# A transformer block kernel: norm columns as stationary operand, x in fewer transfers, modulation issued a block earlier

## The chip, the cores and the metric

The kernel runs on one core of a Trainium2 chip. The metric is the device time of one execution in microseconds (us), lower being better; it is given as the median of several runs. One further execution was recorded by the hardware profiler, and all rows of the trace come from that one.

## The reference

One layer of a diffusion backbone over 512 latent tokens, with 256 context tokens as a prefix, width 1024, all in fp32. Cut to what matters here:

```python
def rmsnorm(x, g):
    return x * lax.rsqrt(jnp.mean(x * x, axis=-1, keepdims=True) + EPS) * g

mod = jax.nn.silu(c) @ w_mod + b_mod                 # c_ctx likewise
sh1, sc1, gt1, sh2, sc2, gt2 = jnp.split(mod, 6)
h = rmsnorm(x, g_norm_mix) * (1.0 + sc1) + sh1       # x: 512 x 1024
hc = rmsnorm(ctx, g_norm_mix) * (1.0 + csc1) + csh1  # ctx: 256 x 1024
mix = token_mixer(h, hc, ...)   # h @ w_in, attention and a gated recurrence, @ w_out
x = x + gt1 * mix
h2 = rmsnorm(x, g_norm_ffn) * (1.0 + sc2) + sh2
x = x + gt2 * swiglu(h2, w_gate, w_up, w_down)
return rmsnorm(x, g_final)
```

The norm needs, for every token, the root of a mean over the 1024 features, and the modulation needs a product of a vector with the matrix `w_mod` before the first large product, `h @ w_in`, can begin.

## The kernel before, in words

Activations lie transposed, with features on the 128 partitions and tokens along the free axis: `xs` is x as 8 blocks (k) of 128 features by 512 tokens, `xc` the context as 8 blocks of 256 tokens. Each large product is made of three (`mm3`, lines 148 to 152: L150, L151, L152): operands are split into a rounded high part and a low part (`hh` and `hl` for h, `gh` and `gl` for the context, `wh` and `wl` for weights). A weight unit of 128 x 1024 is loaded by DMA into `wf`; ACT casts it to `wh` (L132) and DVE subtracts to get `wl` (L133).

**The start.** TensorE runs 32 idle products on a tile of ones (`warm`, L351). x comes in eight transfers (L255, L256), then the modulation weights `wms`, weight units and the context in the order of a written list (L267). ACT squares each block of x (L307) and DVE adds it to the accumulator `acl` (L309). The sum over the 128 partitions is a product on TensorE: the accumulator, 128 tokens at a time, is the stationary operand, two columns of ones move (`rstd_sums`, L174), so each group of 128 tokens gets its sum as one column. `rstd_cols` makes 1/root from it: ACT takes the square root (L190), DVE the reciprocal and one Newton step that ends in L182. To have the value of each token on all partitions, `rstd_diag` multiplies the identity matrix with each column (L209 on DVE, L207 on ACT, in turn), and `rstd_spread` multiplies that diagonal from the left with ones (L216), into a PSUM bank.

**The modulation.** `modvec(k)` multiplies two weight tiles for block k with the vectors of c and c_ctx (eight products on bands of 32 partitions, L320) and copies the result to an SBUF tile `spk` or `modsb` in turn (L323). `modsel(k)` picks the bands by two small products with a selection matrix (L329) and makes scale and shift, `ab`, in three DVE steps (the group L332 is one of them). `make_h` then makes block k of h: DVE multiplies x by scale and 1/root (L339), ACT adds the shift and rounds to `hh` (L340), DVE subtracts to get `hl` (L341).

**The value projection.** The loop from L376 (`g0`) runs over the eight blocks of 128 features. Each has twelve 512-column products, for four groups of 128 tokens (`big` banks, token groups 0 to 3), written in three calls of `g0_mm`. Between them stand, for the next block, `modsel` and `make_h`, and `modvec` for the one after. The context is squared at k = 1, its norm is at k = `lag` - 2 and `lag` - 1 with `lag` = 4, its blocks of h follow two per step, and its products lag four steps behind. The order on each engine is not this order alone: a scheduler in the framework places instructions by priorities and estimated times, so that the code's order and an engine's differ. When the loop ends, the banks are copied out and the other projections, the attention, the recurrence, the output projection and the FFN follow.

**Later norms.** `norm2` (L960) norms x behind the output projection, in two halves of 256 tokens, beside products of the output projection and the FFN. `final` (L1041) norms the result; for the second half it is the last thing that the kernel does: sums, `rstd_cols`, `rstd_diag`, spread, eight multiplications on DVE and the transfers out.

Of the kernel before, what the change touches and what calls it, by code (L numbers as in the profile page):

```python
# [10 lines left out]
F32 = mybir.dt.float32  # L11
# [3 lines left out]
AF = mybir.ActivationFunctionType  # L15
ALU = mybir.AluOpType
AX = mybir.AxisListType

P = 128
# [33 lines left out]
def block_kernel(ctx: ExitStack, tc: tile.TileContext, xT, ctxT, vec, cin, cst, msk, wm, wmt, wi, wqkv, wo, wgu, wd, out):  # L53
# [8 lines left out]
    def nm(s):  # L62
        uid[0] += 1
        return f"{s}_{uid[0]}"
# [137 lines left out]
    def rstd_diag(tp, cols):  # L202
        r, nb = cols
        dg = tp.tile([P, 4, P], F32, tag="rs_d", name=nm("rsd"), bufs=1)
        for b in range(nb):
            if b % 2:
                nc.scalar.activation(dg[:, b, :], ident, AF.Copy, scale=r[:, b : b + 1])  # L207
            else:
                nc.vector.tensor_scalar(dg[:, b, :], ident, r[:, b : b + 1], None, op0=ALU.mult)  # L209
        return dg, nb  # L210

    def rstd_spread(diag):
        dg, nb = diag
        pb = sm()
        for b in range(nb):
            nc.tensor.matmul(pb[:, b * P : (b + 1) * P], ones, dg[:, b, :], start=True, stop=True,  # L216
                             skip_group_check=True)
        return pb

    def rstd_bcast(tp, sqs, ntok, dim, fast=False):  # L220
        return rstd_spread(rstd_diag(tp, rstd_cols(tp, rstd_sums(sqs, ntok), dim, fast)))
# [33 lines left out]
    for k in range(KT):  # L255
        nc.sync.dma_start(xs[:, k, :], xT[:, k, :])  # L256
# [47 lines left out]
    def squares(src, acc_, n):  # L304
        for k in range(KT):
            sq_ = temp(n) if k else acc_
            nc.scalar.activation(sq_, src[:, k, :], AF.Square)  # L307
            if k:
                nc.vector.tensor_add(acc_, acc_, sq_)  # L309

    squares(xs, acl, NL)
# [37 lines left out]
    def warm(n):  # L349
        for _ in range(n):  # L350
            nc.tensor.matmul(pw[:, :P], ones, ones, start=True, stop=True, skip_group_check=True)  # L351
# [12 lines left out]

# [10 lines left out]
    lag = 4  # L375
    for k in range(max(KT, lag + KT // 2)):  # L376
        if k < KT:
            g0_mm(k, (0,))
        if k + 1 < KT:
            abs_.append(modsel(k + 1, sb))  # L380
            make_h(xs, rl, NL, k + 1, abs_[k + 1], 0, hh, hl)
# [4 lines left out]
        if k == lag - 1:  # L386
            rc = rstd_spread(rstd_diag(A, ccols))
# [653 lines left out]
    def final(a):  # L1041
        w = 256
        dg = rstd_diag(N2, rstd_cols(N2, rstd_sums(sqa[a], w), DM, fast=True))
        yield
        pb = rstd_spread(dg)
# [119 lines left out]
```

## Time and profile before

| | us |
|---|---|
| median of three runs | 793.04 (790.87 to 794.18) |
| profiled execution | 792.44 |
| its span in the trace | 790.6 |
| start up to 20.9 | 20.9, TensorE busy 17.10 |
| 20.9 to 71.4, value projection | 50.5, TensorE busy 47.79 |
| 71.4 to 780, all the rest but the tail | 708.6, TensorE busy 700.07 |
| 780 to 790.6, tail | 10.6, TensorE busy 2.02 |

The profiled execution takes 1.84 us more than its span, before the first and behind the last instruction that the trace shows. PE is TensorE, PEld its weight load, DVE VectorE, ACT ScalarE, POOL GpSimd, SP the engine that issues most transfers. A row of the timeline gives start and duration in us, engine, line, operation, out<-in by the program's names, shape and count; in square brackets the idle time of the engine just before it and the instruction that ended it. An fp32 product shows as two passes, so that four products read x8. A row of the windows view gives for each engine the busy time and the count of instructions, then the clock that was granted to TensorE (1.00 is full speed), the share of DMA engines busy and GB/s. A row of the groups gives the shape, the count, the busy time in all and the mean in ns, then the idle time before and who ended it.

### The profile page before, as it was taken

How to read it: one execution, taken by the hardware profiler on the slowest of the kernel's cores; microseconds unless marked ns; L12 is line 12 of the kernel's file. 1: busy time of each engine (PE TensorE's matmuls, PEld its weight loads, DVE VectorE, ACT ScalarE, POOL GpSimd, SP SyncE). 2: the span in 40 equal slices, each digit the busy share in tenths (PEclk: the TensorE clock that was granted, in tenths of full speed). 3: DMA queues.
4: the chain of work that ended last, by engine and by line, in shares of the span. 5: the costliest groups of instructions: out<-in, count | busy, mean ns of one | idle time of the engine just before them, and what ended most of it. 6: DMA issues, size and time to landing. Idle time of an engine off the chain costs nothing.

```text
span 790.6 us, 10838 instructions
## 1 busy us (share of the span) xinstructions
PE 767.0 (97%) x4342; PEld 630.8 (80%) x4342; DVE 445.0 (56%) x819; ACT 307.2 (39%) x564; POOL 10.1 (1%) x18
## 2 busy tenths in 40 slices
PE   8899999999999989999999999999999999999995
PEld 7568878788887768888999888888888888888885
DVE  4686569739778988984566434432333233223324
ACT  5344245434554576664344223222322222212211
POOL 0000000000000100000000000000000000000000
PEclk8999999999999999999999999999999999999997
DMA  8924723321110022453503354423232333332303
GB/s 326 396 82 142 238 81 107 133 67 61 48 55 28 28 96 98 133 166 148 160 2 107 107 159 133 149 92 107 80 107 82 104 78 96 93 100 82 111 2 107
DMA packets 26708, 88.78 MB, mean 112 GB/s; under 512 B 2977, under 2 KB 5281, under 8 KB 26530
## 3 DMA queue, kind: packets, MB, share of 16 engines
q1 hardware_dynamic: 25570, 87.04, 33.5%
q10 hardware_dynamic: 1088, 1.05, 0.4%
q8 instruction: 34, 0.56, 0.3%
q14 instruction: 16, 0.13, 0.0%
HBM read 85.97 MB, written 2.10 MB: 111 GB/s over the span
## 4 chain that ended last, share of the span: by engine, by line
PE 86%; DVE 7%; DMA 4%; ACT 2%; issue 1%; SPq 0%; DVEq 0%; ACTq 0%
PE big L150 17%; PE big L151 16%; PE big L152 16%; PE sm L150 9%; PE sm L151 9%; PE sm L152 9%; PE big L861 2%; DMA xc<-in_ctxT_dram 1%; PE sm L606 1%; DMA wm<-in_wm_dram 1%; PE big L862 1%; DMA wms<-in_wm_dram 1%; PE sm L880 1%; DVE U L587 1%; PE sm L600 1%
## 5 line engine op out<-in xcount | busy, mean ns | idle before, releaser
L133 DVE TENSOR_TENSOR wl<-wf,wh 128x1024 fp32r<-128x1024 f32 (+2 forms) x100 | 119.6, 1196 | 184.5 <-ACT wh L132 184.3
L132 ACT CAST wh<-wf 128x1024 fp32r<-128x1024 f32 (+2 forms) x100 | 102.9, 1029 | 279.8 <-PE big L151 167.4
L150 PE MATMUL big<-h2h,wh 128*128 128x512 f32 (+1 forms) x368 | 140.3, 381 | 0.0
L151 PE MATMUL big<-h2l,wh 128*128 128x512 f32 (+1 forms) x368 | 140.0, 381 | 0.0
L152 PE MATMUL big<-h2h,wl 128*128 128x512 f32 (+1 forms) x368 | 140.0, 381 | 0.0
L151 PEld LDWEIGHTS big<-h2l,wh 128*128 128x128 f32 x368 | 69.2, 188 | 14.6
L152 PEld LDWEIGHTS big<-h2h,wl 128*128 128x128 f32 x368 | 69.2, 188 | 14.5
L150 PEld LDWEIGHTS big<-h2h,wh 128*128 128x128 f32 x368 | 69.2, 188 | 14.4
L150 PE MATMUL sm<-ah,wh 128*128 128x512 f32 (+1 forms) x198 | 73.5, 371 | 0.0
L152 PE MATMUL sm<-ah,wl 128*128 128x512 f32 (+1 forms) x198 | 73.4, 371 | 0.0
L151 PE MATMUL sm<-al,wh 128*128 128x512 f32 (+1 forms) x198 | 73.4, 370 | 0.0
L427 DVE SCALAR_TENSOR_TENSOR wl<-wl,cs 128x1024 f32<-128x1024 f32 x32 | 39.0, 1220 | 35.0 <-DMA wl<-in_wmt_dram 35.0
L150 PEld LDWEIGHTS sm<-ah,wh 128*128 128x128 f32 x198 | 37.3, 188 | 7.1
L151 PEld LDWEIGHTS sm<-al,wh 128*128 128x128 f32 x198 | 37.3, 188 | 7.1
L152 PEld LDWEIGHTS sm<-ah,wl 128*128 128x128 f32 x198 | 37.3, 188 | 7.1
L150 PE MATMUL big<-hh,wh 128*128 128x512 f32 x104 | 42.8, 411 | 0.0
L150 PE MATMUL big<-wh,hh 128*128 128x512 f32 x96 | 39.4, 414 | 3.3 <-ACT hh L340 1.9
L151 PE MATMUL big<-hl,wh 128*128 128x512 f32 x104 | 40.9, 394 | 0.0
L152 PE MATMUL big<-hh,wl 128*128 128x512 f32 x104 | 40.9, 393 | 0.0
L151 PE MATMUL big<-wl,hh 128*128 128x512 f32 x96 | 38.2, 400 | 0.0
L152 PE MATMUL big<-wh,hl 128*128 128x512 f32 x96 | 38.1, 399 | 0.0
L508 DVE RECIPROCAL G<-S 128x528 f32<-128x528 f32 x8 | 27.5, 3433 | 0.1
(320 smaller groups left out, 1345.9 us busy)
## 6 DMA issues: line engine op xcount, KB each, us to landing
wf<-in_wgu_dram SPq DMA_DIRECT2D x44, 512.0 KB, 3.4
wl<-in_wmt_dram SPq DMA_DIRECT2D x32, 512.0 KB, 3.5
wf<-in_wi_dram SPq DMA_DIRECT2D x25, 512.0 KB, 4.2
wf<-in_wd_dram SPq DMA_DIRECT2D x16, 512.0 KB, 3.5
wms<-in_wm_dram SPq DMA_DIRECT2D x11, 512.0 KB, 9.6
wf<-in_wo_dram SPq DMA_DIRECT2D x8, 512.0 KB, 3.3
wf<-in_wd_dram SPq DMA_DIRECT2D x8, 384.0 KB, 3.1
wm<-in_wm_dram SPq DMA_DIRECT2D x5, 512.0 KB, 10.2
```

What stands on the lines that cost most here:

```text
L132: nc.scalar.copy(hi[:, :w], f[:, :w])
L133: nc.vector.tensor_sub(lo[:, :w], f[:, :w], hi[:, :w].bitcast(F32))
L150: nc.tensor.matmul(o, lh, rh, start=start, stop=False, skip_group_check=True)
L151: nc.tensor.matmul(o, lh, rl, start=False, stop=False, skip_group_check=True)
L152: nc.tensor.matmul(o, ll, rh, start=False, stop=stop, skip_group_check=True)
L427: nc.vector.scalar_tensor_tensor(f, f, 1.0, sc, op0=ALU.mult, op1=ALU.mult, accum_out=acc)
L508: nc.vector.reciprocal(I, S)
L587: nc.vector.scalar_tensor_tensor(U[:, c1, :], U[:, c0, :], er[:, 1, c0 : c0 + 1], U[:, c1, :], op0=ALU.mult, op1=ALU.add)
L600: nc.tensor.matmul(t, a2[:, j, :], vt[:, j, h * P : (h + 1) * P], start=True, stop=False, skip_group_check=True)
L606: nc.tensor.matmul(t[g * CH : (g + 1) * CH, :], qg[:, c, :], U[:, c, :], start=False, stop=(g == 1 and d == 1), skip_group_check=True, til ...
L861: nc.tensor.matmul(ps[:, 0, :], L, R[:, :NL], start=(i == 0), stop=(i == 4), skip_group_check=True)
L862: nc.tensor.matmul(ps[:, 1, :NC], L, R[:, NL:], start=(i == 0), stop=(i == 4), skip_group_check=True)
```

## The change

Six edits go together.

1. The diagonals are gone. `rstd_spread` takes the column of 1/root itself as the stationary operand, the same column repeated 128 times (a broadcast view), and the identity moves. The result is the same spread. It applies in all norms (start, context, `norm2`, `final`).
2. x comes in four transfers of two blocks, not eight of one; in the list of later loads the second weight unit comes one place earlier (102 ahead of 6 and -1).
3. The eighth square of x isn't added on DVE; `rstd_sums` takes accumulator and last square, so that TensorE adds them: eight products, not four.
4. Modulation: the code gets `next_h` (selection and h of the next block) and `next_mod` (the next vector), and in blocks 0 and 1 each is called a second time, so that from block 1 on they are a block further ahead.
5. The context's products lag five steps, not four, and its norm moves with them.
6. Idle products: 30, not 32, ahead of the sums (`warm`), two between the first vector and its selection, and five behind the spread (`warm_on`, which multiplies a given tile with ones into a bank that nobody reads).

```diff
-    def rstd_spread(diag):
-        dg, nb = diag
+    def rstd_spread(cols):
+        r, nb = cols
         pb = sm()
         for b in range(nb):
-            nc.tensor.matmul(pb[:, b * P : (b + 1) * P], ones, dg[:, b, :], start=True, stop=True,
+            nc.tensor.matmul(pb[:, b * P : (b + 1) * P], r[:, b : b + 1].to_broadcast([P, P]), ident, start=True, stop=True,
                              skip_group_check=True)
...
-    for k in range(KT):
-        nc.sync.dma_start(xs[:, k, :], xT[:, k, :])
+    for k in range(0, KT, 2):
+        nc.sync.dma_start(xs[:, k : k + 2, :], xT[:, k : k + 2, :])
...
-    for step in (2, 101, 4, 6, -1, 102, 8, -2, 10, 12, 103, 14, 16):
+    for step in (2, 101, 4, 102, 6, -1, 8, -2, 10, 12, 103, 14, 16):
...
             nc.scalar.activation(sq_, src[:, k, :], AF.Square)
+            if last and k == KT - 1:
+                return sq_
...
-    warm(32)
-    cols = rstd_cols(A, rstd_sums([acl], NL), DM, fast=True)
-    sb = modvec(0)
-    dg = rstd_diag(A, cols)
-    abs_ = [modsel(0, sb)]
-    pb = rstd_spread(dg)
+    def warm_on(t, n):
+        for _ in range(n):
+            nc.tensor.matmul(pw[:, :P], ones, t, start=True, stop=True, skip_group_check=True)
+
+    warm(30)
+    cols = rstd_cols(A, rstd_sums([acl, sql], NL), DM, fast=True)
+    sbs = [modvec(0)]
+    warm_on(sbs[0][:, :P], 2)
+    abs_ = [modsel(0, sbs[0])]
+    pb = rstd_spread(cols)
+    warm_on(cols[0][:, 0:1].to_broadcast([P, P]), 5)
     make_h(xs, pb, NL, 0, abs_[0], 0, hh, hl)
     nc.scalar.copy(rl, pb)
-    sb = modvec(1)
...
+    def next_h():
+        k = len(abs_)
+        if k < KT:
+            abs_.append(modsel(k, sbs[k]))
+            make_h(xs, rl, NL, k, abs_[k], 0, hh, hl)
+
+    def next_mod():
+        if len(sbs) < KT:
+            sbs.append(modvec(len(sbs)))
...
-    lag = 4
+    lag = 5
     for k in range(max(KT, lag + KT // 2)):
         if k < KT:
             g0_mm(k, (0,))
-        if k + 1 < KT:
-            abs_.append(modsel(k + 1, sb))
-            make_h(xs, rl, NL, k + 1, abs_[k + 1], 0, hh, hl)
+        if k >= 1:
+            next_h()
...
             g0_mm(k, (1,))
-            if k + 2 < KT:
-                sb = modvec(k + 2)
+            next_mod()
             g0_mm(k, (2, 3))
+            if k < 2:
+                next_h()
+                next_mod()
...
     def final(a):
         w = 256
-        dg = rstd_diag(N2, rstd_cols(N2, rstd_sums(sqa[a], w), DM, fast=True))
+        cols = rstd_cols(N2, rstd_sums(sqa[a], w), DM, fast=True)
         yield
-        pb = rstd_spread(dg)
+        pb = rstd_spread(cols)
```

`norm2` changes like `final`. What follows shows how the instructions stand on three stretches; the numbers in the names tell one buffer from another. Lines of the changed code have moved: the warm-up is L340, `warm_on` L344, the modulation vector L309, the selection L318, the spread L206, a square L294.

TensorE from the warm-up to the first product of the value projection, before:

```order
L351 MATMUL sm_25_194<-ones_63 128x128 x32
L174 MATMUL sm_26_227<-ones_63,acl_168 128x2 x4
L320 MATMUL sm_30_241<-wms_1_77,csil_94 32x256 x8
L329 MATMUL sm_32_256<-cs_61,spk_76 128x2 x2
L216 MATMUL sm_34_263<-rsd_31_251,ones_63 128x128 x4
L320 MATMUL sm_36_273<-wms_1_77,csil_94 32x256 x4
L150 MATMUL big_38_284<-wh_7_110,hh_85 128x512
```

and of the change, from the last two of the eight sums on:

```order
L174 MATMUL sm_26_220<-ones_63,acl_164 128x2
L174 MATMUL sm_26_220<-ones_63,t512_24_183 128x2
L309 MATMUL sm_30_238<-wms_1_77,csil_94 32x256 x8
L344 MATMUL sm_25_189<-spk_76,ones_63 128x128 x2
L318 MATMUL sm_31_250<-cs_61,spk_76 128x2 x2
L206 MATMUL sm_33_257<-cs_61,rsr_29_231 128x128 x4
L344 MATMUL sm_25_189<-rsr_29_231,ones_63 128x128 x5
L309 MATMUL sm_37_280<-wms_1_77,csil_94 32x256 x4
L150 MATMUL big_35_272<-wh_7_106,hh_85 128x512
```

Two idle products now stand between the vector and its selection, and five between the spread and the second vector's first half; the spread reads `rsr`, the column, where it read `rsd`, the diagonals.

TensorE from block 0 to block 1 of the value projection, before (`big_38` and `big_39` are the banks, `modsb_37` the copied vector of block 1):

```order
L152 MATMUL big_38_284<-wh_7_110,hl_86 128x512
L150 MATMUL big_38_284<-wh_7_110,hh_85 128x512
L151 MATMUL big_38_284<-wl_8_111,hh_85 128x512
L329 MATMUL sm_40_289<-cs_61,modsb_37_282 128x2 x2
L152 MATMUL big_38_284<-wh_7_110,hl_86 128x512
L152 MATMUL big_39_285<-wh_7_110,hl_86 128x512
L320 MATMUL sm_42_302<-wms_2_78,csil_94 32x256 x4
L150 MATMUL big_39_285<-wh_7_110,hh_85 128x512
L151 MATMUL big_39_285<-wl_8_111,hh_85 128x512
L152 MATMUL big_39_285<-wh_7_110,hl_86 128x512
L320 MATMUL sm_42_302<-wms_3_79,csil_94 32x256 x4
L150 MATMUL big_38_284<-wh_7_110,hh_85 128x512
```

and of the change, where the banks are `big_35` and `big_36` and the vector is `modsb_38`:

```order
L309 MATMUL sm_37_280<-wms_2_78,csil_94 32x256 x3
L151 MATMUL big_36_273<-wl_8_107,hh_85 128x512
L152 MATMUL big_36_273<-wh_7_106,hl_86 128x512
L150 MATMUL big_36_273<-wh_7_106,hh_85 128x512
L151 MATMUL big_36_273<-wl_8_107,hh_85 128x512
L152 MATMUL big_36_273<-wh_7_106,hl_86 128x512
L318 MATMUL sm_39_297<-cs_61,modsb_38_289 128x2 x2
L309 MATMUL sm_41_307<-wms_2_78,csil_94 32x256 x4
L309 MATMUL sm_41_307<-wms_3_79,csil_94 32x256 x4
L150 MATMUL big_35_272<-wh_7_106,hh_85 128x512
```

The selection for block 1 stood behind seven products of block 0, five of them following it; now all twelve stand ahead of it, and only the two halves of a vector lie between it and the first product of block 1.

ACT around the context norm, before (`wh_14` is the third weight unit, of which block 4 makes the first use, `acc` the context's accumulator and later its spread):

```order
L340 ACTIVATE hh_85<-t512_53_383,ab_52_379 128x512
L190 ACTIVATE rsr_57_392<-sm_54_387,epst_64 128x2
L207 ACTIVATE rsd_61_431<-cs_61,rsr_57_392 128x128
L388 COPY acc_169<-sm_62_434 128x256
L340 ACTIVATE hh_85<-spk_76,ab_60_424 128x512
L340 ACTIVATE gh_87<-sp256_75,ab_33_259 128x256
L340 ACTIVATE gh_87<-sp256_75,ab_41_292 128x256
L132 CAST wh_14_135<-wf_13_133 128x1024
```

and of the change:

```order
L329 ACTIVATE hh_85<-t512_49_373,ab_48_369 128x512
L294 ACTIVATE sp256_75<-xc_93 128x256
L329 ACTIVATE hh_85<-spk_76,ab_55_399 128x512
L190 ACTIVATE rsr_64_445<-sm_61_440,epst_64 128x2
L132 CAST wh_14_131<-wf_13_129 128x1024
L329 ACTIVATE hh_85<-t512_60_436,ab_59_432 128x512
L390 COPY acc_165<-sm_72_491 128x256
```

The cast of that unit stood behind the context's spread and two of its blocks; now it stands right behind the square root of the context's norm, which waits for the context's sums.

More of the change, by code (lines that the diff above doesn't have):

```diff
@@ L200, in rstd_cols @@
         return r, n
-    def rstd_diag(tp, cols):
+    def rstd_spread(cols):
         r, nb = cols
[L204 to L210, printed above, removed]
-    def rstd_spread(diag):
-        dg, nb = diag
         pb = sm()
         for b in range(nb):
-            nc.tensor.matmul(pb[:, b * P : (b + 1) * P], ones, dg[:, b, :], start=True, stop=True,
+            nc.tensor.matmul(pb[:, b * P : (b + 1) * P], r[:, b : b + 1].to_broadcast([P, P]), ident, start=True, stop=True,
                              skip_group_check=True)
         return pb
-    def rstd_bcast(tp, sqs, ntok, dim, fast=False):
-        return rstd_spread(rstd_diag(tp, rstd_cols(tp, rstd_sums(sqs, ntok), dim, fast)))
     D = pool("D", "right")
@@ L303, in block_kernel, with squares @@
     acc = A.tile([P, NC], F32, name="acc")
-    def squares(src, acc_, n):
+    def squares(src, acc_, n, last=False):
         for k in range(KT):
@@ L307, in squares @@
             nc.scalar.activation(sq_, src[:, k, :], AF.Square)
+            if last and k == KT - 1:
+                return sq_
             if k:
                 nc.vector.tensor_add(acc_, acc_, sq_)
-    squares(xs, acl, NL)
+    sql = squares(xs, acl, NL, last=True)
     rl, rc = acl, acc
@@ L386, in block_kernel @@
         if k == lag - 1:
-            rc = rstd_spread(rstd_diag(A, ccols))
+            rc = rstd_spread(ccols)
             nc.scalar.copy(acc, rc[:, :NC])
@@ L1042, in final @@
         w = 256
-        dg = rstd_diag(N2, rstd_cols(N2, rstd_sums(sqa[a], w), DM, fast=True))
+        cols = rstd_cols(N2, rstd_sums(sqa[a], w), DM, fast=True)
         yield
-        pb = rstd_spread(dg)
+        pb = rstd_spread(cols)
         for n in range(KT):
```

## The prediction

> **What bounds the kernel now.** I read the page first, then the windows view, then the timeline of the first 72 us and of the last 10. The page: how busy TensorE is, and the clock it was granted.
>
> ```profile
> span 790.6 us, 10838 instructions
> PE 767.0 (97%) x4342; PEld 630.8 (80%) x4342; DVE 445.0 (56%) x819; ACT 307.2 (39%) x564; POOL 10.1 (1%) x18
> PEclk8999999999999999999999999999999999999997
> ```
>
> TensorE is busy for 97% of the span. The change edits the first 70 us and the two later norms, so its worth is the TensorE time not lost there, plus the tail. The profiled execution took 792.44 us: the span of 790.6 and 1.84 around it. It lies 0.6 below the median of the runs, 793.04. About 0.5% (4.0 us) is what a measurement of this kernel can tell from no change, so "faster" means below 789.1 and "slower" above 797.0.
>
> The windows view of stretches cut where the granted clock changes; the columns are the stretch, its length, busy us of PE, PEld, DVE, ACT and POOL, then clock, DMA share and GB/s.
>
> ```profile
> 10.22:13.63 3.41, 1.80 (x17) 1.61 (x16) 2.22 (x4) 2.42 (x3) 0.00 (x0) 1.00 1.02 419
> 13.63:17.04 3.41, 2.86 (x23) 1.51 (x22) 1.54 (x8) 1.89 (x4) 0.00 (x0) 0.50 1.03 413
> 17.04:20.46 3.42, 3.27 (x18) 2.16 (x18) 1.61 (x5) 0.35 (x1) 0.00 (x0) 0.50 1.03 412
> 34.11:37.52 3.41, 2.12 (x12) 1.49 (x10) 2.53 (x9) 1.14 (x2) 0.00 (x0) 1.00 1.03 410
> 778.21:781.62 3.41, 2.06 (x18) 1.89 (x16) 1.39 (x5) 0.68 (x2) 0.00 (x0) 1.00 0.78 257
> 8.00:10.00 2.00, 2.00 (x20) 2.00 (x19) 1.71 (x3) 1.87 (x4) 0.00 (x0) 1.00 1.03 357
> ```
>
> The clock is halved for two stretches of 3.41 us, 13.63 to 20.46, and comes back. The stretch ahead of them had 1.80 us of busy TensorE, but 0.8 of that are two-column sums. 34.11 to 37.52 was hardly busier (2.12), with 512-column products, and kept the clock. 778.21 to 781.62 had 2.06, half of it two-column sums, and the page's last slice shows the clock lower. I read from this that two-column products hardly hold the clock up.
>
> The timeline of the norm of x, up to the first projection product (start, duration, instruction, idle before and who ended it):
>
> ```profile
> 1.06 10.13 PE L351 MATMUL sm<-ones 128*128 128x128 f32 x64 [1.06 <-DVE epst L90]
> 10.78 0.63 ACT L307 ACTIVATE t<-xs 128x512 f32<-128x512 f32 x1
> 11.27 0.69 DVE L309 TENSOR_TENSOR acl<-acl,spk 128x512 f32<-128x512 f32 x1
> 12.06 0.69 DVE L309 TENSOR_TENSOR acl<-acl,t 128x512 f32<-128x512 f32 x1
> 12.81 1.15 PE L174 MATMUL sm<-ones,acl 128*128 128x2 f32 x8 [1.61 <-DVE acl L309]
> 13.89 1.93 PE L320 MATMUL sm<-wms,csil 128*32 128x256 f32 x16
> 14.96 0.16 DVE L182 SCALAR_TENSOR_TENSOR rsr<-rst,rsr 128x4 f32<-128x4 f32 x1
> 15.89 0.42 DVE L323 COPY spk<-sm 128x256 f32<-128x256 f32 x1 [0.76 <-PE sm L320]
> 16.23 0.47 DVE L209 TENSOR_SCALAR rsd<-cs,rsr 128x128 f32<-128x128 f32 x2
> 16.37 1.01 PE L329 MATMUL sm<-cs,spk 128*128 128x2 f32 x4 [0.55 <-DVE spk L323]
> 17.24 2.05 PE L216 MATMUL sm<-rsd,ones 128*128 128x128 f32 x8
> 19.33 0.75 DVE L339 SCALAR_TENSOR_TENSOR t<-xs,ab,sm 128x512 f32<-128x512 f32 x1 [1.43 <-PE sm L216]
> 20.11 0.72 ACT L340 ACTIVATE hh<-t,ab 128x512 fp32r<-128x512 f32 x1 [3.33 <-DVE t L339]
> 20.89 0.73 PE L150 MATMUL big<-wh,hh 128*128 128x512 f32 x2 [0.58 <-ACT hh L340]
> ```
>
> What ends last is the modulation vector's products at half clock (1.93), its copy, the selection (1.01), the spread (2.05), then 1.6 of DVE and ACT. The projection starts at 20.89.
>
> From there to the end of the value projection the timeline has three waits of TensorE; the other rows give unit prices at full clock:
>
> ```profile
> 26.42 0.50 PE L150 MATMUL big<-wh,hh 128*128 128x512 f32 x1
> 31.01 0.49 PE L150 MATMUL big<-wh,hh 128*128 128x512 f32 x1 [1.08 <-ACT wh L132]
> 37.41 0.50 PE L150 MATMUL big<-wh,hh 128*128 128x512 f32 x1 [1.29 <-ACT hh L340]
> 38.68 0.52 PE L174 MATMUL sm<-ones,acc 128*128 128x2 f32 x4
> 39.13 1.07 PE L320 MATMUL sm<-wms,csil 128*32 128x256 f32 x16
> 41.62 0.60 PE L216 MATMUL sm<-rsd,ones 128*128 128x128 f32 x4
> 45.29 0.73 PE L150 MATMUL big<-wh,hh 128*128 128x512 f32 x2 [0.34 <-ACT wh L132]
> 47.33 0.39 PE L152 MATMUL big<-wh,hl 128*128 128x512 f32 x1
> 47.56 0.39 PE L150 MATMUL big<-wh,hh 128*128 128x512 f32 x1
> 71.41 0.39 PE L150 MATMUL big<-wh,hh 128*128 128x512 f32 x1
> ```
>
> The waits are 1.08 + 1.29 + 0.34 = 2.7 us; after 45.29 there is none up to 71.41, where the next projection follows without a gap. A 512-column product takes a slot of 0.23 (47.33 to 47.56).
>
> **The change part by part.** *x in four transfers, last square to TensorE.* The sums may start once the sixth addition and the eighth square are done, 11.96 (11.27 + 0.69) with the landings as they are, not 12.81. The DMA moves 357 GB/s while x comes in and 419 in the stretch behind: 2.1 MB takes 5.0 instead of 5.9 us at that rate. Against it, after the last landing two squares of 0.63 follow instead of one. I take 0.4 earlier, 11.6 (11.2 to 12.1). The sums are eight products instead of four. Two cost 0.45 (38.68 to 39.13), so eight cost 1.8 and the sums end at 13.65 against 13.96: what the addition saved goes mostly into the products.
>
> *The diagonals go.* The spread waits for the column alone, not for L209. But the new order puts the copy of the modulation vector ahead of the last Newton step on DVE, and two idle products between copy and selection. At full clock: modulation products 13.6 to 14.65, copy to 15.15, idle products 0.45, selection 0.5 to 16.1, spread 1.06 to 17.15, L339 and L340 with their gaps 1.6: the first projection product at 18.8. At half clock from 13.63 on: 1.93 to 15.6, copy to 16.1, two idle products 0.85 to 17.0, selection 0.85, spread 2.05, 1.6: 21.5. A column read 128 times as the stationary operand is in no row. I price it like L216; at twice that the four products cost 1.06 more, and those at the end 0.5; nothing below L216 is expected, since the same columns pass.
>
> *Idle products.* The warm-up is two products shorter, and until 13.6 only two-column sums follow it, a longer thin stretch than now. So I expect the clock halved at about 13.6 again. Then the modulation products and two idle ones fill 1.93 + 0.85 = 2.8 us of the next 3.41. That is nearer to the stretch from 17.04, where 2.05 of spread and 0.9 of modulation products brought the clock back, than to the 1.93 that did not. With the clock back at 17.04: 17.0 + 0.5 + 1.06 + 1.6 = 20.2. Behind the spread stand five more idle products and four modulation products ahead of the projection. At full clock they take 5 x 0.22 + 0.57 = 1.7 and so lie under the 1.6 of L339 and L340; at half clock they take 2.1 + 1.0 = 3.1, and the 21.5 becomes 23.0. Gain of the start: **-0.7** (from -2.1 to +2.1).
>
> The Trainium skill, page "TensorE: Matmul & The Clock Gate", section "HAM oscillation — how this bites in real kernels", says that the clock falls only after gaps of more than about 3.4 us. By that rule the sum would start at 18.8. The trace disagrees: a wait of 1.61 us (row 12.81), with two-column sums behind it, preceded the drop.
>
> *Modulation a block further ahead.* The block's other instructions are the same in number; what counts is where they stand. The prices per block are the rows of these groups (count, busy, mean ns):
>
> ```profile
> L133 DVE TENSOR_TENSOR wl<-wf,wh 128x1024 fp32r<-128x1024 f32 x7 | 8.5, 1218 | 0.4 <-ACT wh L132 0.4
> L332 DVE TENSOR_SCALAR ab<-sm,vc 128x2 f32<-128x2 f32 x8 | 1.7, 218 | 7.5 <-PE sm L329 7.5
> L132 ACT CAST wh<-wf 128x1024 fp32r<-128x1024 f32 x7 | 7.3, 1038 | 2.7 <-PE sm L152 2.7
> ```
>
> Block 0 now takes 26.42 - 20.89 = 5.53 us. In the new order the selection for block 1 stands behind all twelve products of block 0, where five stood behind it. Behind it come three DVE steps (0.55), L339 (0.75), L340 (0.72) and their hand-overs, 2.4 us, and TensorE has only one modulation vector (1.07) to hide it: a wait of 1.25. A group of four modulation products is also cut into one and three, 0.5. The wait for the cast at 31.01 goes, since that cast now stands ahead of block 1's own step on ACT; the one at 37.41 goes too. Before block 4 two new ones come. The selection for block 5 needs a copy that stands on DVE behind block 4's whole chain: 0.55 + 0.75 + 0.72 + 0.74 + 0.42 = 3.2 us, against 2.2 us of products: 1.0. Then the cast of the third weight unit stands on ACT behind the square root of the context norm, which needs sums that TensorE has just begun. The drain of 0.25, the root 0.26 and the cast 1.04 with nothing on TensorE make 1.4 with the hand-overs. New waits 1.25 + 0.5 + 1.0 + 1.4 = 4.1 against 2.7: **+1.4** (-2.7 if all go and none come, +2.5 if a further one follows). The transfers don't decide here: the casts wait in the order of ACT, and the stream of weights is at most earlier. The lag of 5 moves the last twelve context products behind block 7. They fill TensorE either way: 0.
>
> *The later norms.* The one behind the output projection lies beside TensorE work that never stops: 0. At the end it is bare:
>
> ```profile
> 782.22 0.16 DVE L182 SCALAR_TENSOR_TENSOR rsr<-rst,rsr 128x2 f32<-128x2 f32 x1
> 782.42 0.29 DVE L209 TENSOR_SCALAR rsd<-cs,rsr 128x128 f32<-128x128 f32 x1
> 782.85 1.19 PE L216 MATMUL sm<-rsd,ones 128*128 128x128 f32 x4 [1.62 <-DVE rsd L209]
> ```
>
> The spread can start at 782.45 instead of 782.85: **-0.4** (-0.5 to +0.1).
>
> Sum: -0.7 + 1.4 - 0.4 = +0.3, so 792.7 for an execution like the profiled one; with the 0.6 by which that lies below the median, 793.3. What is gained in the norm is given back in the first four blocks.
>
> **The rivals.** *The clock stays up.* Two-column sums hold it after all, or only a stretch without any product lowers it. For: 34.11 to 37.52 was little busier. Against: 778.21 to 781.62, which had 2.06 us and dropped. Start at 18.8, so -2.1 + 1.4 - 0.4 = -1.1, and 793.04 - 1.1 = 791.9.
>
> *The blocks run through as well.* Clock up, and the three waits go while none come, because the vectors are ready early. For: the vector of block 1 is complete long before it is needed. Against: the order on DVE and ACT as worked out. -2.1 - 2.7 - 0.4 = -5.2: 787.8 from the median.
>
> *Slower: the idle products run at half clock.* If the clock drops a stretch earlier, when the warm-up ends on a less lucky edge, all eight sums run at 0.43 a product (3.4 us, to 15.0). Modulation 1.93 (17.0), copy 0.5, idle 0.85, selection 0.85, spread 2.05: 21.2. Then the five idle products and the four of the modulation stand ahead of the projection, 3.1, longer than the 1.6 that they were to fill: 24.3, so +3.4. It decides from the point where TensorE is thin for most of a stretch ending before 13 and the idle products don't bring the clock back before the spread. +3.4 + 1.4 - 0.4 = +4.4; with the 0.6 of the median and 0.2 for block 0's first products at half clock, 797.6. For: eight sums instead of four stay thin for longer. Against: the edges of the profiled run.
>
> **How the numbers follow.** Forecast 0.52 (791 to 795.5 with its own bounds), clock up 0.20, blocks run through 0.12, slower 0.16. The faster share is the third case and a little of the second, 0.13; the slower one is most of the fourth, 0.14; the rest, 0.73, is within 0.5%. Leaving out about a tenth at each end gives 788.0 to 797.6.
>
> **What would show it.** Right: a clock of 0.50 in one or two stretches between 10 and 20 us; the first projection product near 20; its second block waiting over 1 us for ACT hh; before block 4 a wait of over 1 us for the cast; the value projection ending 0 to 2 us from 71.4; the last spread 0.4 us behind the Newton step. Wrong: no clock below 1.00 before 20 us, or the value projection ending before 68.5 or after 75.

## The result and the profile after

The changed kernel takes 798.68 us (median of seven, 795.96 to 798.99), before 793.04 beside it; the ratio is 1.0054, with a 95% interval of 1.0032 to 1.0077 (that of the two medians alone would be 1.0071). In a later repeat it was 1.0029 (1.0010 to 1.0048). By the ratios it is slower by 0.3 to 0.5%. The forecast had +0.3 us; the profiled execution, 795.96 against 792.44, is 3.5 us longer. It was the fastest of its seven.

The page of the changed kernel: the span, the engines' busy time, and the granted clock in 40 slices.

```profile
span 794.2 us, 10842 instructions
PE 769.8 (97%) x4360; PEld 632.9 (80%) x4360; DVE 442.9 (56%) x811; ACT 303.4 (38%) x557; POOL 10.1 (1%) x18
PEclk8999999999999999999999999999999999999997
```

The span grew by 3.6. Share and clock hide it at this grain. The windows view shows where it went; the two long rows are the start and the value projection, the others the stretches around a change of clock.

```profile
0.00:22.02 22.02, 17.88 (x126) 16.02 (x127) 9.66 (x31) 11.71 (x20) 0.53 (x5) 0.84 0.92 344
10.76:14.17 3.41, 2.24 (x24) 2.14 (x28) 1.01 (x2) 1.81 (x4) 0.00 (x0) 1.00 1.03 414
14.17:21.00 6.83, 6.30 (x39) 5.26 (x30) 2.76 (x11) 1.37 (x3) 0.00 (x0) 0.50 1.02 406
22.02:75.06 53.04, 49.77 (x288) 33.33 (x285) 34.61 (x80) 19.60 (x34) 1.95 (x6) 0.97 0.45 169
44.90:48.31 3.41, 2.12 (x16) 1.19 (x17) 3.01 (x7) 1.87 (x3) 0.00 (x0) 1.00 0.00 0
48.31:51.72 3.41, 3.41 (x15) 1.66 (x14) 1.16 (x6) 0.00 (x0) 0.00 (x0) 0.50 0.83 268
```

The start is 22.02 - 20.89 = 1.13 longer, the value projection 53.04 - 50.52 = 2.52, and all behind it 0.1 shorter (719.1 against 719.2). As before, the clock is halved for 6.83 us at the start. New is a third half-clock stretch, 48.31 to 51.72, worth half of 3.41, 1.7 us.

The timeline of the start:

```profile
11.93 0.38 PE L174 MATMUL sm<-ones,acl 128*128 128x2 f32 x2 [2.55 <-DVE acl L298]
13.81 1.64 PE L309 MATMUL sm<-wms,csil 128*32 128x256 f32 x16
15.49 0.42 DVE L312 COPY spk<-sm 128x256 f32<-128x256 f32 x1 [0.64 <-PE sm L309]
15.97 1.22 PE L344 MATMUL sm<-spk,ones 128*128 128x128 f32 x4 [0.53 <-DVE spk L312]
16.98 0.85 PE L318 MATMUL sm<-cs,spk 128*128 128x2 f32 x4
17.70 2.06 PE L206 MATMUL sm<-cs,rsr 128*128 128x128 f32 x8
19.54 1.98 PE L344 MATMUL sm<-rsr,ones 128*128 128x128 f32 x10
20.57 0.72 ACT L329 ACTIVATE hh<-t,ab 128x512 fp32r<-128x512 f32 x1 [5.46 <-DVE t L328]
21.45 0.64 PE L309 MATMUL sm<-wms,csil 128*32 128x256 f32 x8
22.02 0.73 PE L150 MATMUL big<-wh,hh 128*128 128x512 f32 x2
```

The sums start 0.88 earlier (11.93 against 12.81), but the eight end so late that the vector starts at 13.81 against 13.89. The copy gains 0.4 (15.49 against 15.89); the two idle products take 1.0 of TensorE ahead of the selection, and the spread starts 0.46 later than before. It takes 2.06 against 2.05: the repeated column costs nothing of its own. `hh` is ready at 20.57 + 0.72 = 21.29, and the first product waits for TensorE's own queue: five idle products up to 21.5, then the half vector. That is 0.7 more.

Of the value projection, the rows with a wait, the two rows of ACT that the last wait hangs on, and the first row behind its end:

```profile
29.03 0.50 PE L150 MATMUL big<-wh,hh 128*128 128x512 f32 x1 [1.12 <-ACT hh L329]
44.28 0.61 PE L318 MATMUL sm<-cs,modsb 128*128 128x2 f32 x4 [0.87 <-DVE modsb L312]
45.38 0.26 ACT L190 ACTIVATE rsr<-sm,epst 128x2 f32<-128x2 f32 x1 [2.27 <-PE sm L174]
45.54 1.03 ACT L132 CAST wh<-wf 128x1024 fp32r<-128x1024 f32 x1
46.62 0.73 PE L150 MATMUL big<-wh,hh 128*128 128x512 f32 x2 [1.28 <-ACT wh L132]
75.06 0.39 PE L150 MATMUL big<-wh,hh 128*128 128x512 f32 x1
```

The three waits of before are gone and three others are there: 1.12 + 0.87 + 1.28 = 3.27 against 2.71. With the 1.7 of the clock that makes 2.27 of the 2.52. The cast stands behind the root of the context norm, as forecast. Of the last two waits, that of 0.87 ends at 44.28, just ahead of the stretch 44.90 to 48.31, and that of 1.28 lies in it; TensorE is busy for 2.12 of it, in part with two-column products, and the clock falls at its end.

The tail, the last Newton step and the spread behind it:

```profile
786.27 0.16 DVE L182 SCALAR_TENSOR_TENSOR rsr<-rst,rsr 128x2 f32<-128x2 f32 x1
786.58 1.19 PE L206 MATMUL sm<-cs,rsr 128*128 128x128 f32 x4 [1.30 <-DVE rsr L182]
```

The spread starts 0.31 behind the step's start, where before it was 0.63.

### The profile page after: what moved, and what is told of

The parts are those of the page before. It is cut to its first block, busy times and chain, and to the rows that moved or that the text cites. A ratio compares the mean times of both kernels' runs of the same rounds, so it can differ in the third digit from the quotient of the medians.

```text
span 794.2 us, 10842 instructions
## 1 busy us (share of the span) xinstructions
PE 769.8 (97%) x4360; PEld 632.9 (80%) x4360; DVE 442.9 (56%) x811; ACT 303.4 (38%) x557; POOL 10.1 (1%) x18
## 4 chain that ended last, share of the span: by engine, by line
PE 89%; DVE 7%; ACT 2%; issue 1%; DMA 1%; SPq 0%; DVEq 0%; ACTq 0%
PE big L150 17%; PE big L151 17%; PE big L152 17%; PE sm L151 9%; PE sm L150 9%; PE sm L152 9%; PE big L865 2%; PE sm L610 1%; PE sm L309 1%; PE big L866 1%; PE sm L884 1%; DVE U L591 1%; PE sm L604 1%; PE sm L174 1%; PE sm L206 1%
## 5 line engine op out<-in xcount | busy, mean ns | idle before, releaser
L133 DVE TENSOR_TENSOR wl<-wf,wh 128x1024 fp32r<-128x1024 f32 (+2 forms) x100 | 119.6, 1196 | 188.7 <-ACT wh L132 188.6
```

The costliest lines, as they stand in the source:

```text
L133: nc.vector.tensor_sub(lo[:, :w], f[:, :w], hi[:, :w].bitcast(F32))
```

## The experiments

The theory: what the change loses, it loses by waits that the new order puts into the value projection, and by half-clock stretches behind stretches in which TensorE is thinly used. The main rivals: the idle products, which run at half clock, carry the loss; or the repeated column does. All ratios are to the kernel before on the same chip, with 95% intervals.

### Each part alone

The spread alone: the edit of part 1 in the kernel before. `rstd_diag` hands the columns through there, so that `dg` is the column.

```diff
-            nc.tensor.matmul(pb[:, b * P : (b + 1) * P], ones, dg[:, b, :], start=True, stop=True,
+            nc.tensor.matmul(pb[:, b * P : (b + 1) * P], dg[:, b : b + 1].to_broadcast([P, P]), ident, start=True, stop=True,
```

> The kernel before with the spread alone changed: the column of 1/root is the repeated stationary operand in all norms, no diagonals. In the trace of the changed kernel the start's spread took 2.06 us against 2.05 and the last spread started 0.31 us behind the Newton step against 0.63. Theory (the loss comes from the order of the blocks and from the clock): -0.4 us at the tail, 0 at the start, where the selection stands ahead of the spread; ratio 0.998 to 1.001. Rival (the repeated column costs something that the profile does not show as its own): +1 us or more, ratio over 1.001.

Measured: 794.38, ratio 0.9996 (0.9976 to 1.0016). No cost of the column; 0.4 us is too little to be seen in this.

The order alone (parts 4 and 5 in the kernel before):

```diff
-    lag = 4
+    lag = 5
...
-        if k + 1 < KT:
-            abs_.append(modsel(k + 1, sb))
-            make_h(xs, rl, NL, k + 1, abs_[k + 1], 0, hh, hl)
+        if k >= 1:
+            next_h()
...
+            if k < 2:
+                next_h()
+                next_mod()
```

> The kernel before with the order of the modulation alone changed (selection, h and vectors a block further ahead, lag 5). Theory (the loss is in the blocks): a wait of 1.1 to 1.6 us ahead of block 1 and one of about 1 us ahead of block 4, 2.1 to 2.6 us in all where before has 2.7, and a stretch of 3.41 us at half clock behind the waits, 1.7 us: +1 to +3 us, ratio 1.001 to 1.004. Rival (the loss comes from the idle products): the order by itself gains the waits of before, 0 to -2.7 us, ratio 0.9965 to 1.000.

Measured: 796.63, ratio 1.0027 (1.0008 to 1.0045), as the theory had it. The waits of its value projection in the timeline and, in the windows view, the two stretches that matter:

```profile
30.57 0.58 PE L329 MATMUL sm<-cs,spk 128*128 128x2 f32 x4 [0.84 <-DVE spk L323]
36.06 0.50 PE L151 MATMUL big<-wl,hh 128*128 128x512 f32 x1 [0.58 <-DVE wl L133]
40.91 0.50 PE L150 MATMUL big<-wh,hh 128*128 128x512 f32 x1 [0.48 <-ACT hh L340]
47.38 0.61 PE L329 MATMUL sm<-cs,modsb 128*128 128x2 f32 x4 [0.87 <-DVE modsb L323]
50.49 0.80 PE L151 MATMUL big<-wl,hh 128*128 128x512 f32 x1 [0.91 <-DVE wl L133]
```

```profile
12.89:26.54 13.65, 12.52 (x54) 7.66 (x54) 4.57 (x14) 3.08 (x6) 0.00 (x0) 0.50 1.03 410
21.64:77.61 55.97, 52.27 (x284) 34.33 (x285) 35.13 (x82) 20.83 (x36) 1.94 (x6) 0.93 0.44 169
```

The first stands ahead of block 1, as the change's does, but ends with the copy of a vector, not with `hh`; that of 0.87 is the change's. The cast stands ahead of the context's root here, and the wait is then for its low part on DVE. The five make 3.68, more than the 2.1 to 2.6 expected. The half-clock stretches are four at the start in this execution, 12.89 to 26.54, where before has two with nearly the same start, and one behind the waits. This execution took 798.69, 2.1 above the median, and the verdict rests on the ratio.

The idle products alone (part 6 in the kernel before):

```diff
-    warm(32)
+    warm(30)
...
+    warm_on(sb[:, :P], 2)
...
+    warm_on(cols[0][:, 0:1].to_broadcast([P, P]), 5)
```

> The kernel before with the idle products alone (30 ahead, two behind the first vector, five behind the spread). Theory that they cost at half clock: the five and the half vector stand ahead of the first product with 2.6 us at half clock against 1.6 us of work on DVE and ACT, and the two delay the selection by 0.85 us: the first product of the projection 1.5 to 2 us later, ratio 1.002 to 1.0025. Rival (they hold the clock up): no clock of 0.50 ahead of 20 us, or one stretch less, and the first product 0.5 to 2 us earlier, ratio 0.9975 to 0.9995.

Measured: 794.26, ratio 0.9992 (0.9975 to 1.0008). The first product of the projection is late, at 22.37, by the 1.5 of the theory, and two stretches are at half clock as before; but the value projection is 49.2 us long instead of 50.5, since the second vector stands whole ahead of it and the waits are shorter (2.44 in all, before 2.71). So the time did not come as either side had it: put into the kernel before, the idle products cost nothing that can be measured.

x and the last square alone (parts 2 and 3):

```diff
-    for k in range(KT):
-        nc.sync.dma_start(xs[:, k, :], xT[:, k, :])
+    for k in range(0, KT, 2):
+        nc.sync.dma_start(xs[:, k : k + 2, :], xT[:, k : k + 2, :])
...
-    cols = rstd_cols(A, rstd_sums([acl], NL), DM, fast=True)
+    cols = rstd_cols(A, rstd_sums([acl, sql], NL), DM, fast=True)
```

> The kernel before with x in four transfers, the second weight unit one place earlier and the last square summed on TensorE, nothing else. Both theories: the sums start 0.9 us earlier (11.93 in the changed kernel against 12.81) and take 0.85 us longer (eight products at 0.22 against four), so the vector starts 0 to 0.3 us earlier: ratio 0.9990 to 1.0005. If the two-column sums let the clock fall and their longer stretch makes it fall one stretch earlier, +1.7 us: ratio 1.002.

Measured: 796.84, ratio 1.0030 (1.0007 to 1.0052). The first product came earlier, at 20.54, and the kernel was slower all the same. The windows view:

```profile
14.05:24.29 10.24, 9.12 (x50) 5.17 (x43) 5.00 (x15) 3.85 (x7) 0.00 (x0) 0.50 1.03 408
20.54:74.74 54.20, 50.99 (x285) 34.70 (x285) 35.59 (x82) 20.97 (x36) 1.94 (x6) 0.93 0.47 177
```

Three stretches are at half clock from 14.05 on, where before has two: 24.29 - 20.54 = 3.75 us of them lie in the value projection, which before has at full clock throughout, and another stretch lies behind its waits, at 48.18, although the order is that of before (the mean clock of the second row, 0.93, takes in both). That asked for a test of the sums.

### The order undone, and the thin sums

The changed kernel with before's order in the value projection:

```diff
-    lag = 5
+    lag = 4
...
-        if k >= 1:
-            next_h()
+        if k + 1 < KT:
+            abs_.append(modsel(k + 1, sb))
+            make_h(xs, rl, NL, k + 1, abs_[k + 1], 0, hh, hl)
...
-            if k < 2:
-                next_h()
-                next_mod()
```

> The changed kernel with the order of before in the value projection (lag 4, vector and selection one block ahead); all else of the change stays. A run's time is read as its base (time less what the granted clock took, span times one less the mean clock) and the clock's loss. Before had 784.8 + 9.7, the changed kernel 786.6 + 11.4, the order alone 786.3 + 10.3, x and last square alone 785.0 + 11.4. Theory (the order costs 1.6 to 1.9 of base, and x with the last square costs some 1.5 us of clock): base 784.5 to 785.2, clock loss 10.5 to 12. Rival (idle products at half clock ahead of the projection carry the base): base 786 or more.

Measured: 793.77, ratio 1.0003 (0.9985 to 1.0022). Without the new order the rest of the change costs nothing that can be measured, though the interval overlaps with that of the repeat with the order in (1.0010 to 1.0048). Nor is its value projection free of half clock. The stretch with its wait of 0.57 for a cast, and the next:

```profile
45.06:48.47 3.41, 2.72 (x20) 1.43 (x17) 3.32 (x8) 1.85 (x4) 0.00 (x0) 1.00 0.00 0
48.47:51.88 3.41, 3.41 (x15) 1.90 (x14) 2.08 (x6) 1.74 (x3) 0.00 (x0) 0.50 0.73 220
```

The split into base and loss came out against the expectation: base 786.5, loss 7.9. It isn't a clean one, since half-clock time counts as loss also where TensorE waits for others, and then a higher clock only makes the base longer. What follows rests on the ratios and the traces.

Then the sums at the start with 128 moving columns instead of two (w is 128), in before and in the changed kernel:

```diff
-                nc.tensor.matmul(pss[:, 2 * b : 2 * b + 2], s[:, b * P : (b + 1) * P], ones[:, 0:2],
+                nc.tensor.matmul(pss[:, w * b : w * b + w], s[:, b * P : (b + 1) * P], ones[:, 0:w],
```

> The kernel before; the column sums of x at the start move 128 columns of ones, not two (one column of each result is read), nothing else. Theory (sums of two columns hardly count as work, so the clock falls behind them): the sums take about as long (0.22 a product), and the clock's loss falls by one or two stretches of 1.7 us in most runs: loss 6 to 8.5 instead of 9.7, ratio 0.995 to 0.999. Rival (the clock falls because of the wait of 1.6 to 3.4 us for the accumulator ahead of the sums): loss unchanged within 0.7, ratio 0.999 to 1.001.

> The changed kernel with the same wide sums at the start (eight products of 128 columns), nothing else. Theory (eight sums of two columns make the thin stretch longer, and that is what x with the last square costs): clock loss 7 to 9 instead of 11.4, base as in the changed kernel, 786.4 to 786.9, time 794 to 796. Rival (the wait ahead of the sums does it): loss 11 to 12, time unchanged.

And before with a longer warm-up:

```diff
-    warm(32)
+    warm(40)
```

> The kernel before with 40 idle products ahead of the sums, not 32, nothing else. Theory of the thin sums: the loss of clock falls little, 9 to 10. Rival (the wait ahead of the sums lets the clock fall): the wait of 1.6 to 3.4 us shrinks by 1.8, and the loss falls to 6 to 8.5, ratio 0.995 to 0.999. If both the wait and the sums count, each of the two kernels takes a part.

Measured: before with wide sums 792.42, ratio 0.9987 (0.9968 to 1.0007); the changed kernel with wide sums 794.96, ratio 1.0017 (0.9998 to 1.0036), against 1.0054 and 1.0029 with thin ones; before with 40 idle products 792.17, ratio 0.9982 (0.9962 to 1.0002). None is clear of its own kernel by its interval, but each lies below it. Read as base and loss, the loss is 7.1 for both kernels with wide sums and 7.6 with the longer warm-up, where before has 9.1 on that chip; the base of the changed kernel with wide sums came out at 788.0, above the 786.9 of its expectation. The changed kernel with wide sums, timeline and windows view:

```profile
12.58 0.39 PE L174 MATMUL sm<-ones,t 128*128 128x128 f32 x2
12.80 0.39 PE L174 MATMUL sm<-ones,acl 128*128 128x128 f32 x2
```

```profile
10.63:14.05 3.42, 2.12 (x19) 1.93 (x18) 1.39 (x2) 2.04 (x3) 0.00 (x0) 1.00 1.03 418
14.05:20.74 6.69, 5.46 (x55) 3.91 (x54) 3.69 (x12) 2.40 (x5) 0.00 (x0) 1.00 1.03 408
```

A wide sum takes a slot of 0.22 (12.58 to 12.80), as a thin one does with x and the last square alone, and the clock stays up to the first product at 20.74. It falls later all the same: from 44.77 to 51.60, at the waits of 0.87 and 1.29 of the new order. And before with wide sums has one half-clock stretch ahead of the projection (16.60 to 20.02) instead of two, but one in it (43.91 to 47.32). So wide sums alone don't keep the clock throughout.

The stretch 10.63 to 14.05 is busy for 2.12; the change's, with thin sums, was busy for 2.24, and the clock fell behind it. So busy time isn't what the clock goes by. Nor is it the longest gap: with x and the last square alone the clock fell behind the following stretch, busy for 2.93, in which eight thin sums stand and no gap is above 0.49.

```profile
10.63:14.05 3.42, 2.93 (x31) 2.63 (x34) 1.10 (x2) 1.80 (x3) 0.00 (x0) 1.00 1.03 418
```

Of the longer warm-up, the only half-clock stretch ahead of the projection:

```profile
17.36:20.77 3.41, 3.31 (x14) 2.08 (x16) 1.52 (x3) 1.31 (x3) 0.00 (x0) 0.50 1.03 412
```

One stretch, where nine traces with thin sums and 30 or 32 idle products (the two kernels, a repeat, the four parts alone, the old order and the kernel without idle products) have two or more that begin between 12.9 and 14.7. So the wait ahead of the sums counts as well; the rival is true beside the theory.

An estimate from the rows of all fourteen traces brings both under one measure. In each stretch of 3.41 us, add up the columns that TensorE's products move, by the shapes and the modelled times of the rows. A column of an fp32 product counts four times, since 128 of them take the slot (0.22) that 512 take in the value projection (0.23). A product that fills a part of the array counts by that part (the modulation's, 128*32 in their rows, a quarter). Behind 39 stretches at full clock the clock fell: each has at most 3,072 by this count. Behind 3,116 it stayed: each has at least 3,072.

| stretch | count | the clock behind it |
|---|---|---|
| before, 10.22 to 13.63 | 2,078 | fell |
| the change, 10.76 to 14.17, thin sums | 634 | fell |
| the change with wide sums, 10.63 to 14.05 | 4,217 | stayed |
| before, 34.11 to 37.52 | 3,387 | stayed |
| the change, 44.90 to 48.31 | 2,579 | fell |

Waits and two-column products lower the count alike. It also weighs the order, as an estimate. The edges of the stretches lie elsewhere in every execution; move them through all places in steps of 0.1 us, and the value projection of each of the five traces with the new order has a stretch under 3,072 wherever they lie, 1.1 to 2.4 of them on average. The nine traces with before's order have 0 to 0.8. A stretch at half clock costs 1.7 us.

### Combined, and the change again

Before with the repeated column, wide sums at both ends and 40 idle products:

```diff
-    warm(32)
-    cols = rstd_cols(A, rstd_sums([acl], NL), DM, fast=True)
+    warm(40)
+    cols = rstd_cols(A, rstd_sums([acl], NL, P), DM, fast=True)
...
-        dg = rstd_diag(N2, rstd_cols(N2, rstd_sums(sqa[a], w), DM, fast=True))
+        dg = rstd_diag(N2, rstd_cols(N2, rstd_sums(sqa[a], w, P), DM, fast=True))
```

> The kernel before with three edits: the repeated column in the spread, wide sums (128 columns) at the start and in the last norm, 40 idle products ahead of the sums. Theory (TensorE without full products lets the clock fall): at most one stretch of 3.41 us at half clock before the projection's first product, where seven traces with two-column sums and 30 or 32 idle products have two; some 1.7 us from that, 0.4 from the tail's diagonals and 0.5 from a spread at full clock there: 1.5 to 3 us, ratio 0.996 to 0.998. Rival (the clock's loss only moves to the value projection): ratio 0.9985 to 1.0005.

Measured: 790.66, ratio 0.9963 (0.9947 to 0.9979), below the wide sums or the longer warm-up alone (0.9987 and 0.9982), and the first here whose whole interval lies below one. Its windows view (start, then value projection) and its tail in the timeline:

```profile
7.10:20.34 13.24, 10.75 (x105) 8.96 (x103) 7.42 (x18) 7.14 (x11) 0.00 (x0) 1.00 1.01 397
20.34:69.39 49.05, 47.14 (x276) 32.80 (x277) 34.82 (x80) 20.46 (x35) 1.94 (x6) 1.00 0.54 204
```

```profile
780.45 0.16 DVE L182 SCALAR_TENSOR_TENSOR rsr<-rst,rsr 128x2 f32<-128x2 f32 x1
780.76 0.68 PE L209 MATMUL sm<-cs,rsr 128*128 128x128 f32 x4 [1.30 <-DVE rsr L182]
```

No stretch at half clock from 7.10 to 69.39. The last spread takes 0.68 instead of 1.19, at a clock that falls later. The loss did not move on.

The change with before's order, wide sums, 40 idle products ahead and none behind:

```diff
-    warm(30)
+    warm(40)
...
-    warm_on(sbs[0][:, :P], 2)
...
-    warm_on(cols[0][:, 0:1].to_broadcast([P, P]), 5)
```

> The changed kernel with the order of before in the value projection, wide sums at the start, 40 idle products ahead of the sums and none behind. So x comes in four transfers, the last square is summed on TensorE and the column is repeated, as in the change. Theory: the sums of x may start up to 0.9 us earlier with eight wide products and no two-column stretch; projection's first product near 19.5, ratio 0.996 to 0.998. Rival (x with the last square costs by itself, 1.0030 alone, whatever the clock): ratio 1.000 to 1.003.

Measured: 789.89, ratio 0.9955 (0.9939 to 0.9972), the fastest of all, within the interval of the one above. The first product did not come near 19.5, but at 20.70: the 40 idle products run up to 12.70, so that the sums can't start earlier. One stretch in the value projection, 43.76 to 47.17, is at half clock in its trace. x in four transfers, the last square on TensorE and the repeated column are in it: they cost nothing that can be measured once the sums stream.

The change without its idle products:

```diff
-    warm(30)
+    warm(32)
...
-    warm_on(sbs[0][:, :P], 2)
...
-    warm_on(cols[0][:, 0:1].to_broadcast([P, P]), 5)
```

> The changed kernel without its seven idle products behind the sums and with 32 ahead. Theory that they cost at half clock: the first product of the projection 0.8 to 1.5 us earlier than in the changed kernel's trace (22.02), time 0.5 to 1.5 us under the changed kernel of the same chip. Rival (they bring the clock back earlier than the norm would): one stretch of half clock more, time 0.5 to 1.7 us above it.

Measured: 800.09, ratio 1.0083 (1.0057 to 1.0108), against the theory that they cost. The first product came 0.54 earlier than in the repeat below (21.58 against 22.12), and was paid for at block 1. Timeline, then windows view:

```profile
26.77 1.22 DVE L133 TENSOR_TENSOR wl<-wf,wh 128x1024 fp32r<-128x1024 f32 x1
29.72 0.50 PE L150 MATMUL big<-wh,hh 128*128 128x512 f32 x1 [2.25 <-ACT hh L329]
```

```profile
28.00:31.30 3.30, 1.58 (x9) 1.40 (x10) 2.43 (x7) 1.95 (x5) 0.00 (x0) 1.00 1.04 413
31.30:34.72 3.42, 3.42 (x15) 1.65 (x13) 2.54 (x6) 1.75 (x4) 0.00 (x0) 0.50 1.02 407
```

Without them the scheduler puts a unit's subtraction (L133, 1.22) between the selection's steps for block 1, the wait there grows from 1.12 to 2.25, and a half-clock stretch follows. So this run doesn't weigh the idle products by themselves: taking them out also changed the order on DVE. Two more half-clock stretches lie behind the waits ahead of block 4, 48.39 to 55.21. The run shows once more what waits at these places cost.

The change again, with no edit:

> The changed kernel once more, beside the others on one chip. If its slowdown is the order's waits and the clock: ratio 1.003 to 1.007 again, two stretches at half clock before the first product and one or more behind the waits of the value projection. If the first comparison came out high by the luck of where the clock's stretches fell: ratio 1.000 to 1.003.

Measured: 796.16, ratio 1.0029 (1.0010 to 1.0048), just under the theory's 1.003 and still in the range of the rival, so that some of the first 1.0054 may be the luck of where the stretches fell. The traces speak for the theory: its waits in the value projection are 1.12, 0.87 and 1.29 again, and the clock falls at the start and behind the waits. The windows view:

```profile
14.74:21.57 6.83, 6.30 (x37) 5.64 (x30) 3.21 (x10) 1.75 (x4) 0.00 (x0) 0.50 1.03 407
45.40:52.23 6.83, 5.54 (x24) 2.41 (x24) 3.56 (x10) 1.87 (x3) 0.00 (x0) 0.50 0.43 154
```

Two stretches behind the waits this time, one in the first trace: the same waits cost one or two, as the clock's windows fall.

## Why the prediction was right in its waits and wrong in its clock

The sum was +0.3: start -0.7, blocks +1.4, tail -0.4. The trace has start +1.1, blocks +2.5, and the rest -0.1. The median of 798.68 lies 1.1 above the upper end of the range; by the ratio, 1.0054 x 793.04 = 797.3, the change lies just inside it. That is luck more than working: the upper end came from the rival in which all eight sums run at half clock, and they did not. Both numbers lie above the 797.0 from which the forecast counted "slower", which had a chance of 0.14. And the trace that was followed is 2.7 below the median; what its other executions lost beyond it no trace shows.

*The waits of the blocks were right.* Forecast: 1.25 ahead of block 1 for `hh` (its own terms, 2.4 less 1.07, give 1.33), 1.0 for the vector of block 5, 1.4 for the cast behind the context's root, and those of before gone. Measured: 1.12, 0.87, 1.28, and gone. The order alone costs (1.0027), and with the order undone no loss is left that can be measured (1.0003).

*The first step that failed* is the price of those waits. The +1.4 counted idle time alone. The wait of 1.28, with two-column products in the same stretch of 3.41 us, also dropped the clock for the next, 1.7 us; in the repeat two stretches were lost. The working knew the rule from the start of the kernel and did not apply it thirty microseconds later, where the waits that it forecast itself made the stretch thin. With it the blocks would have been +3.1, and the forecast +2.0.

*The second* is "With the clock back at 17.04". It came back at 21.0. The vector and the idle products made the stretch from 14.17 no busier than the one from 13.63 before (2.88 against 2.86). The start's own bound of 21.5 to 23.0 held the 22.02, and the terms behind it were right: five idle products and a half vector at half clock, ahead of the first product. The rival that priced this at 24.3 had this half of the mechanism, but not the other: the clock fell behind the sums, not ahead of them, and the start lost a third of its price.

*The sums.* "What the addition saved goes mostly into the products" was right (13.81 against 13.89). That eight thin products make a longer thin stretch it said too, and put no price on it: alone, x and the last square are 1.0030.

*The clock staying up* (a chance of 0.20) did not happen in the change; with wide sums it does at the start. The Trainium skill, page "TensorE: Matmul & The Clock Gate", section "HAM oscillation — how this bites in real kernels", puts the drop at gaps of over some 3.4 us. The trace disagrees: the longest gap ahead of 48.31 is 1.28 us.

*The tail* was right: 0.31 instead of 0.63 behind the Newton step, 8.38 - 7.93 = 0.45 from the step to the end of the span. The rest behind the value projection shows only 0.1 of it; where the other 0.3 went wasn't followed.

*The offset of 0.6* to the median didn't carry over: the change's profiled execution lies 2.7 below its median, as its other executions had a lower mean clock (0.984 to 0.986 in five of seven, against 0.988).

What stays open: how much of the slowdown is the order and how much the thin sums. Undoing either brings the ratio near one (1.0003, 1.0017, whose intervals overlap with the repeat's), and both act through the clock's stretches, so that their parts needn't add. No run widens the sums of the context norm or the selections, which still move two columns in the value projection.

## What to carry to other kernels

A wait of TensorE of about a microsecond should be priced twice: by itself, and by half of the next 3.4 us if the stretch that it falls into moves few columns. Work that streams only two columns doesn't keep the clock; widening it to 128 columns took no longer here, and with the repeated column and a warm-up that reaches to the first sums it gave 0.9963 and 0.9955, where reordering alone gave 1.0027. Moving work a step ahead in the code helps only if nothing that it needs stands behind a longer chain on another engine: read the order of that engine, too.

## What the runs showed of the hardware

- The clock moves in stretches of 3.41 us, or multiples of it, with a phase that differs from execution to execution: the first drop came at 13.63, 14.17 and 14.7 in three traces of two kernels with nearly the same start. Before, unchanged, took 790.7 to 798.8 us on one chip, at a mean clock of 0.992 to 0.982: eight us for the 1% of clock. Four of the fourteen traces have a half-clock stretch near 270 us, in code that no edit touches.

- A sum with two moving columns and one with 128 take the same slot, 0.22 us. In the changed kernel the clock fell behind the first kind and stayed at 1.00 behind the second, up to the projection.
- A column repeated 128 times as the stationary operand costs what a full matrix does: 2.06 against 2.05 at half clock.
